# A third pair of K tiles as seven products of sums in the down projections of a two-layer trunk

## The chip, the cores and the metric

The kernel runs on one core of a Trainium2 chip. The metric is the device time of one execution in microseconds; lower is better. TensorE (PE) multiplies, VectorE (DVE) and ScalarE (ACT) do the elementwise work, GpSimd (POOL) and SyncE (SP) mostly issue transfers.

## What is computed

A decoder trunk of two layers over 256 rows of width 2048. Layer 0 mixes by a gated spatial unit and a sparse attention, layer 1 by a short gated convolution; each mixer has an input and an output projection. Every layer then has a feed-forward part, and a last norm ends the trunk. The change concerns the last product of this, with `D_FF` = 5632:

```python
def swiglu(h, w_gate, w_up, w_down):
    return (jax.nn.silu(h @ w_gate) * (h @ w_up)) @ w_down
...
        h = h + swiglu(rmsnorm(h, norm_ffn[i]), w_gate[i], w_up[i], w_down[i])
    return rmsnorm(h, norm_f)
```

All is float32. The kernel splits every operand into a rounded high part and a low rest (`h`, `l`; `wh`, `wl`) and forms each product from three matmuls: high by high, high by low, low by high.

## The kernel before

**Blocks and units.** The 256 rows are two row tiles (`MT` = 2, `m`), K goes in tiles of 128, columns in chunks of 512 (`NW`). A *block* (`Stream.block`) computes two chunks of columns at once: gate and up for one chunk of the hidden width, or two chunks of a down projection. Its K runs over 8 pairs of K tiles (6 in the last part). The blocks are cut into *units*, and `Stream.run` goes through them: `multiply(i)` issues the matmuls of unit i, `ahead(i)` splits the weights of the units up to four further on, and `after(i)` runs what was hooked to this unit.

**Two kinds of pairs.** A pair of K tiles by two row tiles by two chunks is, for each chunk, four products of a 128x128 block of the operand with a 128x512 block of weights: eight in all. An ordinary pair is two units ("n", one for each chunk) with 12 matmuls each. The other kind replaces the eight products by seven (Winograd's form of Strassen's scheme): four units ("s") of 2, 2, 2 and 1 products, that is 6, 6, 6 and 3 matmuls. It needs sums of operand blocks and of weight blocks. The weights' sums are made partly by transfers that add into SBUF (issued by POOL in `load`, L184) and partly by two additions on VectorE (`sum2`, L137; `sum4`, L140); the operand's sums are made in `x_split` (L423 to L439). Which pairs are done so says `SUMS`, pairs 4 and 6; the sums live in the tiles `sa`, `sx` (`open_late`, `second_operand`).

**The order.** A string sets the order of a block's units by hand:

```python
    N8 = [(k, k in SUMS) for k in range(8)], "nnnnn sns sns sns sns nnn"
    F8 = [(k, k in (4, 6)) for k in range(8)], "nnnnnn sns sns sns sns nn"
    N6 = [(k, k in SUMS) for k in range(6)], "nnn nn sn sn sn s nn"
```

An "sns sns" is the first, second, third and fourth unit of one seven with two ordinary units between. N8 is used for blocks of eight pairs, F8 for the first block behind a norm, N6 for down blocks of six pairs.

**PSUM.** Ordinary products and four of a chunk's sums accumulate in the four buffers of `pg` (`BANK`). Four products of sums (P1, P5, P6, P7, keys in `FREE`) have banks of their own in `pm`, which has four buffers too, given out in turn; transposes (`transposed_bank`, L370) take theirs from the same four. P1 is opened by the first unit of a block's first seven, P5 and P7 by its second, P6 by its third; all are held until the block's sums are done.

**End of a block.** When the last seven has multiplied its third unit, `summed` (L464) copies P1 out and adds P5 to P7 on VectorE (L472 to L475); a down block adds the two results to `h` (L503). `done` then adds the ordinary banks to `h` (L508), two for the first chunk behind the block's last unit, two for the second behind the first unit of the next block; the next block's first matmul needs the first of these banks.

**Start of a block.** `begun` hooks the preparation of operands: for the down projections `pairs` transposes the product of silu(gate) and up (L1000) behind units 2 and 3 of the next block, two pairs each gate block, and `x_split` turns each one unit later into `y` (`split_T`, L381, L382) or, for pairs in `SUMS`, into `y` and `sx`.

**Parts.** `feed_forward` takes the hidden width in parts of 4, 4 and 3 chunks (`PARTS`): a part's gate and up blocks, then its down blocks, two for all 2048 columns (one in the very last part, whose other columns go by plain `gemm`). That makes 6 + 5 down blocks, 8 of eight pairs and 3 of six.

**Weights.** `load` issues the transfers on SP in the order of the units as buffers come free (8 of `raw`, two of `ts`); `split` makes high and low parts (L205 on ScalarE, L208 on VectorE) in a ring of five buffers (`wh0` to `wh4`): a unit's split can start when the unit five before it has multiplied.

Of the kernel before, what the change touches and what calls it, by code (L numbers as in the profile page):

```python
# [8 lines left out]
F32 = mybir.dt.float32  # L9
BF16 = mybir.dt.bfloat16  # L10
F32R = mybir.dt.float32r
AF = mybir.ActivationFunctionType
# [3 lines left out]
P = 128  # L16
# [17 lines left out]
PROBS, VALUES = 4, 6  # L34
PARTS = (4, 4, 3)
SUMS = {4: 0, 6: 1}
BANK = ((1, 3), (2, 7))
P1, P5, P6, P7 = FREE = (0, 4, 5, 6)


class Operand:

    def __init__(self, h=None, l=None, sh=None, sl=None):
        self.h, self.l, self.sh, self.sl = h, l, sh, sl

    def tile(self, kt, m):
        sl = slice(m * P, (m + 1) * P)
        return self.h[:, kt, sl], self.l[:, kt, sl]  # L50

    def sum(self, kp, i):
        return self.sh[:, SUMS[kp], i], self.sl[:, SUMS[kp], i]


class Stream:
# [44 lines left out]
    def block(self, ws, form, src, begun, summed, done):  # L101
# [6 lines left out]
        for kp, seven in order:  # L108
# [3 lines left out]
            def t(k, m, k0=k0):  # L112
                return lambda: src.tile(k0 + k, m)

            def s(i, kp=kp):
                return lambda: src.sum(kp, i)

            if not seven:
                for n in range(2):
                    queue["n"].append((wk[n], {"frees": 1, "mms": [(k, t(k, m), BANK[n][m]) for m in range(MT)  # L120
                                                                    for k in range(2)]}))
# [3 lines left out]
        for c in pattern.replace(" ", ""):  # L125
# [4 lines left out]
            elif item:  # L130
# [8 lines left out]
                def sum4(ra=ra, rb=rb, ts=ts):  # L139
                    self.nc.vector.tensor_add(ts[0][:, 2], self.raw[rb][:, 0], self.raw[ra][:, 1])  # L140

                sevens = [
                    {"raw": ra, "prep": sums13, "mms": [(0, t(0, 0), P1), (1, t(1, 0), BANK[0][0])]},
                    {"raw": rb, "ts": ts, "at": 0, "then": sum2, "mms": [(0, s(1), P5), (1, s(0), P7)]},
                    {"raw": rb, "then": sum4, "frees": (ra,), "mms": [(0, s(2), P6), (1, s(3), BANK[1][0])]},
                    {"raw": rb, "ts": ts, "at": 2, "w": 1, "mms": [(0, t(1, 1), BANK[0][1])]},
                ]
# [102 lines left out]
    def run(self):  # L250
        n = len(self.units)
        i = 0
        while i < n:
# [9 lines left out]
            if u.get("first"):  # L263
                c["ps"] = [self.bank(k) for k in BANK[self.turn]]
                self.turn ^= 1
# [25 lines left out]
def trunk(ctx: ExitStack, tc: tile.TileContext, x, norm_mix, norm_ffn, norm_f, w_in_ab, w_out_ab, sgu_w, sgu_b,  # L291
          sgu_g, cmp_pe_k, cmp_w1_k, cmp_w2_k, cmp_pe_v, cmp_w1_v, cmp_w2_v, w_in_c, conv_w, w_out_c, w_gate,
          w_up, w_down, out):
    nc = tc.nc
# [10 lines left out]
    st = Stream(nc, raws, parts, (psg, psm))  # L305
# [5 lines left out]
    h = acts.tile([P, MT, D], F32, name="h")  # L311
# [64 lines left out]
    def split_T(banks, dst, kt0, gain):  # L376
        dh, dl = dst
        for b, t in enumerate(banks):
            k0 = kt0 + 2 * b
            if gain is None:  # L380
                nc.scalar.activation(dh[:, k0:k0 + 2, :], t, AF.Copy)  # L381
                nc.vector.tensor_sub(dl[:, k0:k0 + 2, :], t, dh[:, k0:k0 + 2, :].bitcast(F32))  # L382
            else:
                gs = [gain[:, k0 + k:k0 + k + 1] for k in range(2)]
                for k, g in enumerate(gs):
                    nc.scalar.activation(dh[:, k0 + k, :], t[:, k, :], AF.Copy, scale=g)
                for k, g in enumerate(gs):
                    nc.vector.scalar_tensor_tensor(dl[:, k0 + k, :], t[:, k, :], g, dh[:, k0 + k, :].bitcast(F32),
                                                   op0=ALU.mult, op1=ALU.subtract)
# [21 lines left out]
    late = {}  # L411

    def x_split(src, dst, kp, gain=None):

        ks = slice(2 * kp, 2 * kp + 2)
        if kp not in SUMS:
            split_T([src.rearrange("p (k m) c -> p k (m c)", k=2)], (dst.h, dst.l), 2 * kp, gain)
            return
        xs = late["pool"].tile([P, 8, P], F32, name="xs")
        a = xs[:, :4]  # L420
        if gain is not None:
            for k in range(2):
                nc.scalar.activation(a[:, 2 * k:2 * k + 2], src[:, 2 * k:2 * k + 2], AF.Copy,  # L423
                                     scale=gain[:, 2 * kp + k:2 * kp + k + 1])
        elif src.space == bass.MemoryType.PSUM:
            nc.scalar.activation(a, src, AF.Copy)
        else:
            a = src
        v = a.rearrange("p (k m) c -> p k (m c)", k=2)
        nc.vector.tensor_sub(xs[:, 4:6], a[:, 0:2], a[:, 1:4:2])  # L430
        nc.vector.tensor_sub(xs[:, 6], a[:, 0], xs[:, 5])
        nc.vector.tensor_sub(xs[:, 7], a[:, 2], xs[:, 6])

        def parts():
            i = SUMS[kp]
            nc.scalar.activation(dst.h[:, ks], v, AF.Copy)
            nc.scalar.activation(dst.sh[:, i], xs[:, 4:], AF.Copy)
            nc.vector.tensor_sub(dst.l[:, ks], v, dst.h[:, ks].bitcast(F32))
            nc.vector.tensor_sub(dst.sl[:, i], xs[:, 4:], dst.sh[:, i].bitcast(F32))  # L439

        st.at(1, parts)

# [5 lines left out]
    def open_late():  # L448
        next_region()
        pool = late["pool"] = region("late")  # L450
        pool.tile([P, LATE_PAD], F32, name="pad")
        for n in ("a", "x"):
            for x in "hl":
                late[n + x] = pool.tile([P, len(SUMS), 4, P], F32R, name=f"s{n}_{x}")
        src_a.sh, src_a.sl = late["ah"], late["al"]
        st.widen(pool)

    def second_operand():

        src_x.h, src_x.l = (yp.tile([P, KT, S], F32R, name=f"y{i}") for i in range(2))  # L460
        if late:
            src_x.sh, src_x.sl = late["xh"], late["xl"]

    def summed(part, b):  # L464

# [28 lines left out]
    def add_to_h(n2, squares=None):  # L494
# [10 lines left out]
        def done(n, b):  # L505
            for m in range(MT):
                hs = h[:, m, c0 + n * NW:c0 + (n + 1) * NW]
                nc.vector.tensor_add(hs, b[BANK[n][m]], hs)  # L508
            if squares:
# [7 lines left out]
    def region(name, bufs=1):  # L517
        return stage.enter_context(tc.tile_pool(name=name, bufs=bufs, reuse_waits="tile"))

    def next_region():  # L520
        stage.close()
# [59 lines left out]
    src_a, src_x = Operand(a_h, a_l), Operand()  # L581
# [375 lines left out]

    N8 = [(k, k in SUMS) for k in range(8)], "nnnnn sns sns sns sns nnn"
    F8 = [(k, k in (4, 6)) for k in range(8)], "nnnnnn sns sns sns sns nn"
    N6 = [(k, k in SUMS) for k in range(6)], "nnn nn sn sn sn s nn"  # L960
    begun = []

    f0 = norm_from("f0", g_ffn[0])
# [17 lines left out]
        st.gemm(w_out_ab[0], [0, 8, 12, 4], c * NW, src_x, out_ab(c, *f0))  # L981


    def feed_forward(layer, rname, norm):
        c0 = 0
        for part, nb in enumerate(PARTS):
            for c in range(c0, c0 + nb):
                def done(n, b, c=c, kb=4 * c0):
                    g, u = late["g"], late["u"]
                    for m in range(MT):  # L990
                        t = (g, u)[n][:, m]
                        nc.vector.tensor_add(t, b[BANK[n][m]], t)

                    def later():
                        for m in range(MT):
                            r = R[rname][:, m:m + 1]
                            if n == 0:
                                nc.scalar.activation(g[:, m], g[:, m], AF.Silu, scale=r)
                            else:
                                nc.vector.scalar_tensor_tensor(g[:, m], u[:, m], r, g[:, m], op0=ALU.mult, op1=ALU.mult)  # L1000

                    st.at(1, later)

                def pairs(b, c=c, c0=c0):
                    if c == c0 and b == 0:
                        second_operand()
                    x_pair(late["g"], b * S, src_x, 2 * (c - c0) + b)

                st.block([(w_gate[layer], 0, c * NW), (w_up[layer], 0, c * NW)], F8 if c == 0 else N8, src_a, begun[:],
                         summed, done)  # L1010
                begun[:] = [(2, lambda p=pairs: p(0)), (3, lambda p=pairs: p(1))]
            last = part == len(PARTS) - 1
            for n2 in range(2):
                if last and layer == 1 and n2 == 1:
                    break
                sums, done = add_to_h(n2, norm[0] if last else None)
                ws = [(w_down[layer], 4 * c0, 2 * n2 * NW), (w_down[layer], 4 * c0, (2 * n2 + 1) * NW)]
                st.block(ws, N8 if nb == 4 else N6, src_x, begun[:], sums, done)
                begun[:] = norm[1](n2) if last else []
            c0 += nb  # L1020

# [12 lines left out]


    cv = {}
    top = ExitStack()
    wc = w_in_c[0]

    def open_conv():  # L1040
        cv["p"] = top.enter_context(tc.tile_pool(name="convt", bufs=2, reuse_waits="tile"))
        r2 = cv["r2"] = const.tile([P, MT], F32, name="r2")
        nc.vector.tensor_mul(r2, R["c1"], R["c1"])
# [68 lines left out]
    for c in (0, 2):  # L1112
        for cc in (c, c + 1):
            done, then = done_cz(cc)
# [3 lines left out]
        done, then = done_bg(c)  # L1118
# [4 lines left out]
    for n2 in range(2):  # L1123
        sums, done = add_to_h(n2, squares)
# [68 lines left out]
    for c in (2, 3):  # L1193
        w = w_down[1][4 * sum(PARTS[:2]) * P:]
        st.gemm(w, [0, 4, 8], c * NW, src_x, last(c), tail=AHEAD + 1 if c == 3 else 0)
# [61 lines left out]
```

## Time and profile before

| | |
|---|---|
| median of 3 runs | 2150.6 us (2150.55 to 2150.61) |
| the profiled execution | 2150.6 us |
| its span | 2148.9 us |
| PE busy | 2128.4 us, 99% |
| PE weight loads | 1750.3 us, 81% |
| DVE busy | 1610.4 us, 75% |
| ACT busy | 1146.3 us, 53% |
| POOL busy | 161.0 us, 7% |
| DMA | 473.30 MB, mean 220 GB/s |

The profile is of one execution. Busy time of PE counts the matmuls' modelled durations, which overlap, so it tells that PE has work and not how fast it goes. The chain that ended last runs 96% over PE and 1% each over DVE, DMA and issue. Idle time of another engine costs nothing as long as PE doesn't wait for it.

### The profile page before, as it was taken

The page shows a single profiled execution, that of the slowest core. Times are in us where ns is not written, and L with a number is a line of the kernel's source. Part 1 is how long each engine was busy: PE and PEld are TensorE (multiplying, and loading weights), DVE is VectorE, ACT ScalarE, POOL GpSimd, SP SyncE. Part 2 cuts the span into 40 slices and gives each one's busy share as a digit, 9 for nine tenths or more (in the row PEclk, how much of TensorE's full clock was granted, in tenths as well). Part 3 has the DMA queues.
Part 4 walks back from the last instruction along what each step waited for, and adds up shares of the span by engine and source line. Part 5 has one row for each costly group of instructions (what it writes and reads, how often), then busy time and mean ns, then how long its engine had stood idle before and what let it go on. Part 6 is the DMA issues. An engine that isn't in the chain of part 4 may idle for free.

```text
span 2148.9 us, 27123 instructions
## 1 busy us (share of the span) xinstructions
PE 2128.4 (99%) x9663; PEld 1750.3 (81%) x9663; DVE 1610.4 (75%) x1981; ACT 1146.3 (53%) x1411; POOL 161.0 (7%) x217
## 2 busy tenths in 40 slices
PE   9999999999999999999999999999999999999998
PEld 7887788888888888888788888788888888888886
DVE  5567756777777787777788787877877777777776
ACT  6456555555455555455565555555555455544553
POOL 2000000000000100010010000000000000000000
PEclk9999999999999999999999999999999999999999
DMA  8764467777877877886777777777887788778873
GB/s 261 207 187 129 146 204 208 216 240 230 242 219 241 245 226 216 248 244 200 214 234 221 209 248 238 216 223 219 242 241 220 230 244 241 216 230 244 242 220 108
DMA packets 256040, 473.30 MB, mean 220 GB/s; under 512 B 17848, under 2 KB 29552, under 8 KB 255904
## 3 DMA queue, kind: packets, MB, share of 16 engines
q1 hardware_dynamic: 229104, 425.27, 60.4%
q0 software_dynamic: 23136, 42.67, 12.1%
q10 hardware_dynamic: 3664, 3.63, 0.5%
q8 instruction: 76, 1.25, 0.2%
q14 instruction: 60, 0.49, 0.1%
HBM read 469.40 MB, written 2.10 MB: 219 GB/s over the span
## 4 chain that ended last, share of the span: by engine, by line
PE 96%; DVE 1%; issue 1%; DMA 1%; ACT 1%; SPq 0%; POOLq 0%; POOL 0%; DVEq 0%; ACTq 0%
PE pg L229 23%; PE pg L231 22%; PE pg L230 22%; PE pg L238 5%; PE pg L240 5%; PE pg L239 5%; PE pm L231 3%; PE pm L229 3%; PE pm L230 3%; PE pm L370 2%; DVE wl L208 1%; PE pm L757 0%; PE pm L834 0%; DMA h<-in_x_dram 0%; PE pm L623 0%
## 5 line engine op out<-in xcount | busy, mean ns | idle before, releaser
L208 DVE TENSOR_TENSOR wl<-raw,wh 128x1024 fp32r<-128x1024 f32 (+1 forms) x769 | 928.4, 1221 | 423.6 <-ACT wh L205 392.0
L205 ACT ACTIVATE wh<-raw 128x1024 fp32r<-128x1024 f32 (+1 forms) x769 | 804.7, 1058 | 781.8 <-PE pg L231 525.4
L229 PE MATMUL pg<-wh,a_h 128*128 128x512 f32 x1456 | 572.1, 393 | 1.6 <-DVE h L508 1.6
L231 PE MATMUL pg<-wh,a_l 128*128 128x512 f32 x1456 | 567.4, 390 | 0.0
L230 PE MATMUL pg<-wl,a_h 128*128 128x512 f32 x1456 | 566.8, 389 | 0.0
L229 PEld LDWEIGHTS pg<-wh,a_h 128*128 128x128 f32 x1456 | 273.4, 188 | 58.9 <-ACT wh L205 2.0
L231 PEld LDWEIGHTS pg<-wh,a_l 128*128 128x128 f32 x1456 | 273.3, 188 | 57.7
L230 PEld LDWEIGHTS pg<-wl,a_h 128*128 128x128 f32 x1456 | 273.6, 188 | 55.3
L229 PE MATMUL pg<-wh,y 128*128 128x512 f32 x646 | 253.8, 393 | 3.1 <-DVE h L508 3.1
L231 PE MATMUL pg<-wh,y 128*128 128x512 f32 x646 | 251.7, 390 | 0.0
L230 PE MATMUL pg<-wl,y 128*128 128x512 f32 x646 | 251.4, 389 | 0.0
L205 ACT ACTIVATE wh<-ts 128x1024 fp32r<-128x1024 f32 (+1 forms) x158 | 133.8, 847 | 92.2 <-PE pg L231 91.0
L208 DVE TENSOR_TENSOR wl<-ts,wh 128x1024 fp32r<-128x1024 f32 (+1 forms) x158 | 150.6, 953 | 35.6 <-ACT wh L205 35.6
L184 POOL DMA_DIRECT2D ts<-in_w_up_dram x88 | 76.3, 1015 | 947.0 <-DVE ub L475 324.3
L229 PEld LDWEIGHTS pg<-wh,y 128*128 128x128 f32 x646 | 121.3, 188 | 29.7 <-ACT wh L205 3.9
L231 PEld LDWEIGHTS pg<-wh,y 128*128 128x128 f32 x646 | 121.2, 188 | 25.7
L230 PEld LDWEIGHTS pg<-wl,y 128*128 128x128 f32 x646 | 121.4, 188 | 24.6
L238 PE MATMUL pg<-wh,a_h 128*128 128x512 f32 x288 | 121.0, 420 | 0.6 <-ACT wh L205 0.6
L239 PE MATMUL pg<-wl,a_h 128*128 128x512 f32 x288 | 113.1, 393 | 0.8 <-DVE wl L208 0.8
L240 PE MATMUL pg<-wh,a_l 128*128 128x512 f32 x288 | 113.4, 394 | 0.0
L238 PE MATMUL pg<-wh,y 128*128 128x512 f32 x176 | 69.1, 393 | 1.6 <-DVE h L508 1.6
L240 PE MATMUL pg<-wh,y 128*128 128x512 f32 x176 | 68.5, 389 | 0.0
(255 smaller groups left out, 2188.2 us busy)
## 6 DMA issues: line engine op xcount, KB each, us to landing
raw<-in_w_gate_dram SPq DMA_DIRECT2D x176, 512.0 KB, 4.7
raw<-in_w_down_dram SPq DMA_DIRECT2D x157, 512.0 KB, 5.4
raw<-in_w_up_dram SPq DMA_DIRECT2D x132, 512.0 KB, 4.8
raw<-in_w_in_c_dram SPq DMA_DIRECT2D x84, 512.0 KB, 4.8
raw<-in_w_in_ab_dram SPq DMA_DIRECT2D x72, 512.0 KB, 3.9
ts<-in_w_up_dram POOLq DMA_DIRECT2D x88, 256.0 KB, 5.7
raw<-in_w_out_ab_dram SPq DMA_DIRECT2D x32, 512.0 KB, 4.1
raw<-in_w_out_c_dram SPq DMA_DIRECT2D x28, 512.0 KB, 4.7
```

The lines of the kernel that those rows point to most:

```text
L184: self.nc.gpsimd.dma_start(out=ts[0][:, k], in_=wb[:, 0], accum_op=ALU.add)
L205: nc.scalar.activation(hv[:, ks], src[:, ks], AF.Copy)
L208: nc.vector.tensor_sub(lv[:, ks], src[:, ks], hv[:, ks].bitcast(F32))
L229: nc.tensor.matmul(ps, xh, hv[:, j, :], start=uses[0] == (i, x), stop=False)
L230: nc.tensor.matmul(ps, xh, lv[:, j, :], start=False, stop=False)
L231: nc.tensor.matmul(ps, xl, hv[:, j, :], start=False, stop=uses[-1] == (i, x))
L238: nc.tensor.matmul(ps[m], xh, hv[:, k, :], start=u["first"] and k == 0, stop=False)
L239: nc.tensor.matmul(ps[m], xh, lv[:, k, :], start=False, stop=False)
L240: nc.tensor.matmul(ps[m], xl, hv[:, k, :], start=False, stop=u["last"] and k == 1)
L370: nc.tensor.transpose(t[:, k * S + m * P:k * S + (m + 1) * P], src[:, m, c + k * P:c + (k + 1) * P], ident)
```

## The change

In the down projections pair 2 is done as seven products too, beside pairs 4 and 6 (beside 4 where there are six). Its operand sums go into two new tiles `t0`, `t1` from a pool of their own (`third`), opened at the first part of a layer's feed-forward and closed before the convolution's and at the last norm's. The sums of an operand stand in a dictionary by pair. Gate and up, the convolution and its projections keep their forms. The patterns of the down blocks become D8 and D6:

```diff
+THIRD = 2
...
     def sum(self, kp, i):
-        return self.sh[:, SUMS[kp], i], self.sl[:, SUMS[kp], i]
+        h, l = self.sums[kp]
+        return h[:, i], l[:, i]
...
     def x_split(src, dst, kp, gain=None):
-        if kp not in SUMS:
+        if kp not in dst.sums:
...
-    def second_operand():
+    def second_operand(third=None):
         src_x.h, src_x.l = (yp.tile([P, KT, S], F32R, name=f"y{i}") for i in range(2))
         if late:
-            src_x.sh, src_x.sl = late["xh"], late["xl"]
+            src_x.sums = {kp: (late["xh"][:, i], late["xl"][:, i]) for kp, i in SUMS.items()}
+        if third:
+            src_x.sums[THIRD] = third
...
-    N6 = [(k, k in SUMS) for k in range(6)], "nnn nn sn sn sn s nn"
+    D8 = [(k, k in SUMS or k == THIRD) for k in range(8)], "nn sns sns sns sns sns sns nn"
+    D6 = [(k, k in (4, THIRD)) for k in range(6)], "nn sns sns sns sns nn"
...
                     if c == c0 and b == 0:
-                        second_operand()
+                        if c == 0:
+                            top.close()
+                            pool = top.enter_context(tc.tile_pool(name="third", bufs=1, reuse_waits="tile"))
+                            third[:] = [pool.tile([P, 4, P], F32R, name=f"t{i}") for i in range(2)]
+                        second_operand(third)
...
-                st.block(ws, N8 if nb == 4 else N6, src_x, begun[:], sums, done)
+                st.block(ws, D8 if nb == 4 else D6, src_x, begun[:], sums, done)
```

The lines of the changed kernel are 2 to 12 further on: L208 becomes L210, L229 to L231 become L231 to L233, L370 L372, L382 L384, L472 L476, L503 L507, L508 L512, L1000 L1008.

Two places of the order are shown. The first is VectorE's queue at the end of the first down block (layer 0, first part): `wl` are splits of weights, L503 and L508 the additions to `h`. Before:

```order
L474 TENSOR_TENSOR ub<-pm,ga 128x512
L475 TENSOR_TENSOR ub<-pm,ub 128x512
L503 TENSOR_TENSOR h<-h,ga 128x2x512
L503 TENSOR_TENSOR h<-h,ub 128x2x512
L208 TENSOR_TENSOR wl_4970<-raw,wh_4969 128x1024
L208 TENSOR_TENSOR wl_4988<-raw,wh_4987 128x1024
L208 TENSOR_TENSOR wl_5006<-raw,wh_5005 128x1024
L508 TENSOR_TENSOR h<-pg,h 128x512 x2
```

and with the change:

```order
L478 TENSOR_TENSOR ub<-pm,ga 128x512
L479 TENSOR_TENSOR ub<-pm,ub 128x512
L507 TENSOR_TENSOR h<-h,ga 128x2x512
L507 TENSOR_TENSOR h<-h,ub 128x2x512
L210 TENSOR_TENSOR wl_5017<-raw,wh_5016 128x1024
L210 TENSOR_TENSOR wl_5035<-raw,wh_5034 128x1024
L512 TENSOR_TENSOR h<-pg,h 128x512 x2
```

Between the additions of the sums and those of the ordinary banks stand two splits in place of three; the additions of the next block's first seven (L139, L142) come five rows behind.

The second is TensorE's queue at the start of that same block, from the second transpose of the product (L370, then L372) on; `y` are plain operands, `t` the sums of pair 2, `pg` and `pm` the two groups of PSUM banks, and in brackets stands whom a row waits for. Before, an ordinary unit of twelve matmuls follows, of which seven rows stand here:

```order
L370 MATMUL pm<-ident,ga 128x128 x4
L229 MATMUL pg<-wh_4694,y_3684 128x512 [waits Activation_49]
L230 MATMUL pg<-wl_4695,y_3684 128x512
L231 MATMUL pg<-wh_4694,y_3685 128x512
L229 MATMUL pg<-wh_4694,y_3684 128x512
L230 MATMUL pg<-wl_4695,y_3684 128x512
L231 MATMUL pg<-wh_4694,y_3685 128x512
L229 MATMUL pg<-wh_4694,y_3684 128x512
```

With the change the second and third unit of a seven follow: P5, P7 and, with a wait for VectorE, P6:

```order
L372 MATMUL pm<-ident,ga 128x128 x4
L231 MATMUL pm<-wh_4704,t_3687 128x512 [waits Activation_49]
L232 MATMUL pm<-wl_4705,t_3687 128x512
L233 MATMUL pm<-wh_4704,t_3688 128x512
L231 MATMUL pm<-wh_4704,t_3687 128x512 [waits Activation_49]
L232 MATMUL pm<-wl_4705,t_3687 128x512
L233 MATMUL pm<-wh_4704,t_3688 128x512
L231 MATMUL pm<-wh_4725,t_3687 128x512 [waits DVE_49]
L232 MATMUL pm<-wl_4726,t_3687 128x512
```

The first products of a block's first seven have moved from unit 5 to unit 2, before the transposes, and the three banks of P5, P7 and P6 are opened right behind them.

## Rows read from the trace of the kernel before

**Rows 1.** The page's part 1: busy us, share of the span, instructions by engine.

```profile
PE 2128.4 (99%) x9663; PEld 1750.3 (81%) x9663; DVE 1610.4 (75%) x1981; ACT 1146.3 (53%) x1411; POOL 161.0 (7%) x217
```

**Rows 2.** Windows: engine busy us (x instructions), granted clock, DMA share, GB/s.

```profile
533.30:575.80 42.50, 42.50 (x193) 35.19 (x192) 33.85 (x40) 23.77 (x27) 3.40 (x4) 1.00 0.81 234
1036.00:1042.00 6.00, 4.42 (x21) 3.36 (x20) 6.00 (x8) 3.16 (x6) 0.00 (x0) 1.00 0.84 232
```

**Rows 3.** Timeline of PE, end of an N6 block: start us, us, line, operands.

```profile
1034.48 0.39 PE L231 MATMUL pg<-wh,y 128*128 128x512 f32 x1
...
1037.20 0.39 PE L231 MATMUL pg<-wh,y 128*128 128x512 f32 x1
...
1037.88 0.39 PE L231 MATMUL pg<-wh,y 128*128 128x512 f32 x1
1039.85 0.47 PE L229 MATMUL pg<-wh,y 128*128 128x512 f32 x1 [1.57 <-DVE h L508]
```

**Rows 4.** The waits: who waited for whom, us in total, times, longest.

```profile
PE pg L229 <- DVE h L508: 4.7, 3, 1.6
PE pg L238 <- DVE h L508: 1.6, 1, 1.6
```

**Rows 5.** Timeline of DVE, end of the same N6 block.

```profile
1030.69 1.23 DVE L208 TENSOR_TENSOR wl<-raw,wh 128x1024 fp32r<-128x1024 f32 x1 [0.21 <-ACT wh L205]
...
1036.75 2.35 DVE L208 TENSOR_TENSOR wl<-raw,wh 128x1024 fp32r<-128x1024 f32 x2
1039.02 1.28 DVE L508 TENSOR_TENSOR h<-pg,h 128x512 f32<-128x512 f32 x2
```

**Rows 6.** Timeline of DVE, end of an N8 down block.

```profile
572.30 3.49 DVE L208 TENSOR_TENSOR wl<-raw,wh 128x1024 fp32r<-128x1024 f32 x3
575.70 1.28 DVE L508 TENSOR_TENSOR h<-pg,h 128x512 f32<-128x512 f32 x2
```

**Rows 7.** Timeline of PE, the same end.

```profile
576.16 0.39 PE L231 MATMUL pg<-wh,y 128*128 128x512 f32 x1
576.53 0.47 PE L229 MATMUL pg<-wh,y 128*128 128x512 f32 x1
```

**Rows 8.** Timeline of DVE, end of the F8 block of the output projection.

```profile
1379.41 2.35 DVE L208 TENSOR_TENSOR wl<-raw,wh 128x1024 fp32r<-128x1024 f32 x2
```

**Rows 9.** Timeline of PE, the same end.

```profile
1382.51 0.47 PE L229 MATMUL pg<-wh,y 128*128 128x512 f32 x1 [1.57 <-DVE h L508]
```

**Rows 10.** Timeline of all engines, start of an N8 down block.

```profile
544.63 0.60 PE L370 MATMUL pm<-ident,ga 128*128 128x128 f32 x4
...
544.88 1.06 ACT L205 ACTIVATE wh<-raw 128x1024 fp32r<-128x1024 f32 x1 [1.66 <-issue]
...
545.97 1.23 DVE L208 TENSOR_TENSOR wl<-raw,wh 128x1024 fp32r<-128x1024 f32 x1 [0.40 <-ACT wh L205]
...
547.12 0.68 DVE L382 TENSOR_TENSOR y<-pm,y 128x512 fp32r<-128x512 f32 x1
```

**Rows 11.** Timeline of PE, the same start.

```profile
533.26 0.39 PE L229 MATMUL pg<-wh,y 128*128 128x512 f32 x1
...
544.99 0.48 PE L229 MATMUL pg<-wh,y 128*128 128x512 f32 x1
```

**Rows 12.** Timeline of DVE, the same start.

```profile
538.46 1.41 DVE L1000 SCALAR_TENSOR_TENSOR ga<-ub,r_f,ga 128x512 f32<-128x512 f32 x2
...
548.32 0.69 DVE L439 TENSOR_TENSOR sx_l<-xs,sx_h 128x512 fp32r<-128x512 f32 x1
```

**Rows 13.** DMA: queues (packets, MB, share of engines); issues (KB, us to landing).

```profile
q1 hardware_dynamic: 229104, 425.27, 60.4%
q0 software_dynamic: 23136, 42.67, 12.1%
...
ts<-in_w_down_dram SPq DMA_DIRECT2D x38, 256.0 KB, 6.2
ts<-in_w_down_dram POOLq DMA_DIRECT2D x38, 256.0 KB, 6.7
```

More of the change, by code (lines that the diff above doesn't have):

```diff
@@ L41, with __init__ @@
 class Operand:
-    def __init__(self, h=None, l=None, sh=None, sl=None):
-        self.h, self.l, self.sh, self.sl = h, l, sh, sl
+    def __init__(self, h=None, l=None):
+        self.h, self.l, self.sums = h, l, {}
     def tile(self, kt, m):
@@ L434, in parts @@
         def parts():
-            i = SUMS[kp]
+            sh, sl = dst.sums[kp]
             nc.scalar.activation(dst.h[:, ks], v, AF.Copy)
-            nc.scalar.activation(dst.sh[:, i], xs[:, 4:], AF.Copy)
+            nc.scalar.activation(sh, xs[:, 4:], AF.Copy)
             nc.vector.tensor_sub(dst.l[:, ks], v, dst.h[:, ks].bitcast(F32))
-            nc.vector.tensor_sub(dst.sl[:, i], xs[:, 4:], dst.sh[:, i].bitcast(F32))
+            nc.vector.tensor_sub(sl, xs[:, 4:], sh.bitcast(F32))
         st.at(1, parts)
@@ L454, in open_late @@
                 late[n + x] = pool.tile([P, len(SUMS), 4, P], F32R, name=f"s{n}_{x}")
-        src_a.sh, src_a.sl = late["ah"], late["al"]
+        src_a.sums = {kp: (late["ah"][:, i], late["al"][:, i]) for kp, i in SUMS.items()}
         st.widen(pool)
-    def second_operand():
+    def second_operand(third=None):
         src_x.h, src_x.l = (yp.tile([P, KT, S], F32R, name=f"y{i}") for i in range(2))
         if late:
-            src_x.sh, src_x.sl = late["xh"], late["xl"]
+            src_x.sums = {kp: (late["xh"][:, i], late["xl"][:, i]) for kp, i in SUMS.items()}
+        if third:
+            src_x.sums[THIRD] = third
     def summed(part, b):
@@ L981, in trunk @@
         st.gemm(w_out_ab[0], [0, 8, 12, 4], c * NW, src_x, out_ab(c, *f0))
+    top = ExitStack()
+    third = []
     def feed_forward(layer, rname, norm):
@@ L1036, in trunk @@
     cv = {}
-    top = ExitStack()
     wc = w_in_c[0]
     def open_conv():
+        top.close()
         cv["p"] = top.enter_context(tc.tile_pool(name="convt", bufs=2, reuse_waits="tile"))
```

## The prediction, made before the changed kernel had run

> **What bounds the kernel now.** I read the page first. TensorE's matmuls cover 99% of the span [rows 1], and the windows say the clock is granted in full (1.00, the 2.4 GHz level) in the down projections, while VectorE is busy 33.85 of 42.50 us and the DMA engines 0.81 of it [rows 2]. So only two things change the time: the number of matmuls, and the moments when TensorE stands. The pace of the matmuls is in the timeline: the last matmul of one K-pair unit starts at 1034.48 and that of the next at 1037.20, so twelve matmuls of 512 columns take 2.72 us, **0.2267 us each** [rows 3]. The 0.39 us that the rows give as a duration overlaps the next one and is no price.
>
> The waits say where TensorE stands in the chunks with products of sums: four times at a block's end, for `h` of L508, 6.3 us in all [rows 4]. One of them is the row at 1039.85 [rows 3]: that matmul starts 1.97 us after the one before, 1.74 us more than the pace. The timeline of VectorE explains it [rows 5]: the last split before the sums starts at 1030.69, then come the sums of products and their additions to h, from 1036.75 two splits, and only at 1039.02 the additions that free the PSUM banks for the next block. VectorE doesn't idle in this; the order of its queue is what makes TensorE wait. Where three ordinary units stand behind the last product of sums (N8), VectorE does three splits before those additions, from 572.30 [rows 6], and TensorE meets the free bank almost in time: 576.16 to 576.53 is 0.37 us, 0.14 over the pace [rows 7]. The first chunk of the convolution's output projection (F8 with additions to h) ends on two ordinary units and has again two splits and the 1.57 us of idle time [rows 8, 9]. So **the tail "nn" or "nnn" of the pattern decides**, not the layer: one unit less gives TensorE 2.72 us less to do and VectorE one split (1.13 us, half of the time from 1036.75 to 1039.02) less, and the difference, 1.59 us, is the wait that appears.
>
> **The change, part by part.**
>
> *Products.* Each of the 11 down blocks (8 of eight pairs, 3 of six) does one more pair with seven products in place of eight: 3 matmuls fewer, 33 in all, on the path: 33 x 0.2267 = **-7.5 us**. The Trainium skill's page "TensorE: Matmul & The Clock Gate", section "Back-to-back issue gap", gives N/2.4 + 2.5 ns between matmuls, 215.8 ns at 512 columns; by it the term would be an estimated 7.1 us, but the trace's own pace decides.
>
> *Ends of blocks.* N8 ends on "nnn"; D8, which takes its place in 8 down blocks, ends on "nn". The order shows VectorE's queue with two splits before the additions, as at 1036.75. From the end of the last product of sums TensorE has the same units as there (three ordinary ones and the short fourth unit of the seven), so I take the wait seen there: 1.97 in place of 0.37 us between the matmuls, 8 x 1.60 = **+12.8 us**. N6 ended on "nn" already and D6 does too: those 3 blocks keep theirs. Bounds: 0 if VectorE came to its sums earlier; I take the upper end, for three ends of the same shape all show it.
>
> *Starts of blocks.* The first down block of each part (6: four D8, two D6) transposes the last two pairs of y behind its units 2 and 3. `pm` has four buffers. N8 has only ordinary units there; in D8 and D6 unit 2 is already a product and holds a buffer until the block's end, the transposes take two, P5 the fourth, P7 the first transpose's, and **P6, with which unit 5 opens, the second transpose's**. The order shows a wait for VectorE on its first matmul. What that waits for can be timed in the block of before [rows 10]: the second transpose starts at 544.63, when unit 3 ends; ScalarE first splits the weights whose ring slot unit 3 has just freed (544.88), VectorE follows (545.97), and only then comes L382, which reads the transposed bank, from 547.12 to 547.80: 3.17 us after the end of unit 3, with about 0.15 until TensorE starts (the first of the two additions from 1039.02, 0.68 long like L382, lets the matmul go at 1039.85 [rows 3, 5]). TensorE has there only the transposes, 0.36 us until 544.99 [rows 11] with 0.09 more on the next matmul, and the six matmuls of unit 4, 1.36: 1.81 us. The wait is 3.32 - 1.81 = 1.5 us, 6 x 1.5 = **+9.1 us**. Bounds: 0 (the transposed bank is read before the split) and 2.7 (another split of 1.13 stands ahead); the row is the same work in the same order, so I take its value. The first transposes need L1000's product: in before it ends at 539.87, 6.61 us after the block's start at 533.26 [rows 11, 12], and the thirty matmuls of D8's units 0 to 2 end at 6.80: just in time, 0.
>
> *Operands.* Pair 2 of y is made six times as sums: three subtractions and one split more on VectorE, two copies more on ScalarE, in the third gate block of a part, behind units 3 and 4. The down block of before does just this with pair 6 (L439, its last step, ends at 549.0 [rows 12]) and TensorE doesn't wait; N8's five ordinary units cover it. Cost 0; if the cover failed, as much as a start, 6 x 1.5.
>
> *Splits and additions of weights.* A seven needs 3.5 splits of full width where a pair needs 2, and two additions: VectorE 1.5 x 1.23 + 2 x 0.68 = 3.2 us more [rows 5, 10] in a block of some 42, from 33.85 to 37; TensorE's time in that block covers it, since the inner "sns sns" is what before already runs with without a wait. Cost 0, if it is evenly spread; that it isn't is the ends' term.
>
> *Transfers.* A seven loads 0.26 MB more by SP and adds 0.52 MB by POOL. At the queues' rates (425.27 MB in 60.4% of the span, 42.67 MB in 12.1% [rows 13]) that is 0.8 and 3.2 us of all sixteen engines: the share goes from 0.81 to 0.90. `ts` has two buffers, so the third seven of a block must wait for the fourth unit of the first (unit 7), whose split follows the end of unit 2 by 2.5 us at most (544.63 to 547.12 [rows 10]): 9.3 us into the block. The loads take 6.2, the adding transfers 6.7 [rows 13]: 22.2. Unit 16, which uses them, multiplies behind 132 matmuls, at 29.9 + 2.4 for transposes and wait, so its addition and split must begin at 29. So 0, with 6.8 us to spare; from there each us costs 8, at twice the latencies 8 x 6.1 = 49, the bound above.
>
> **Sum:** -7.5 + 12.8 + 9.1 = +14.4 us. The profiled execution took 2150.6 us (span 2148.9), the median of the three runs is the same 2150.6, so the forecast is **2165.0 us**. The new stops are of the length of those that exist; around one of them the clock stays at 1.00 [rows 2], so none is charged for the clock.
>
> **Rivals.**
> - *Only the ends wait* (the transposed bank is read early enough): -7.5 + 12.8 = 2155.9. For it: ScalarE's copy of the bank comes right behind the wait's start. Against: the order has VectorE's split ahead of L384. 12%.
> - *Only the starts wait:* 2152.2. It needs VectorE ahead of the ends by 1.6 us, which no "nn" end of before is. 5%.
> - *Faster: no new wait.* The mechanism is the ring of five split buffers: if the sevens, which begin three units earlier, let VectorE finish the products' sums of the end before the last splits, the additions to h meet TensorE as in N8, and the bank of P6 is met likewise; then the 33 matmuls count in full, 2143.1. The point from which it decides: the first addition of L512 must start before the block's last matmul (575.70 against 576.16 in N8, but 1039.02 against 1037.88 in N6 [rows 3, 5 to 7]). Against it: the last split before the sums waits for a slot that TensorE frees, and its place hasn't moved. 6%.
> - *The third pair of sums comes late.* It needs more than 6.8 us over the measured latencies; a share of 0.90, with bursts in it, speaks for it, the 22.2 against 29 us against. Price: at 8 us over, 1.2 late in 8 blocks, 2165 + 10 = 2175. The Trainium skill's page "SBUF — State Buffer", section "SBUF: two separate sides", has a rule that would bring this about: descriptors of transfers issued by GpSimd can't be written while VectorE, in a two-port mode, holds the ports that both share. No row here shows it: the adding transfers land in 6.7 us beside a VectorE that is busy 80% of the time. 9%.
> - *The change does not do what it says:* the order has 33 matmuls fewer and 22 adding transfers more; excluded.
> The forecast's own case keeps 68%.
>
> **How the numbers follow.** In the forecast's case the ends are 8 x 1.5 to 1.65, the starts 6 x 1.2 to 1.9, so 2162 to 2168.5. The range takes in the rival of the ends alone below and part of late sums above: 2155 to 2171, with the rest (6 + 5 + most of 9%) outside. About 0.2%, 4.3 us, is what a measurement can tell from no change: slower are the forecast, the ends alone (+5.3) and late sums, 89%; the same is 5%; faster 6%.
>
> **What would show it.** Right: 33 matmuls fewer; gaps of 1.97 us at all eight D8 ends with L512 as releaser, twelve waits of that kind in the list in place of four; six gaps of some 1.7 us on the first P6 matmul with L384 as releaser; VectorE near 88% in a D8 block, clock 1.00. Wrong: an end gap of 0.4 us in a D8 block, no wait for L384, or waits for `ts` transfers on VectorE or ScalarE that reach TensorE.

## The result, and the profile of the changed kernel

| | before | after |
|---|---|---|
| median of the runs | 2150.61 us (4 runs, 2150.55 to 2151.02) | 2164.73 us (4 runs, 2164.64 to 2166.34) |
| ratio, 95% interval | | 1.0064 (1.0052 to 1.0077) |
| profiled execution | 2150.6 us, span 2148.9 | 2166.34 us, span 2164.6 |

The change makes the kernel 14.1 us slower by the medians, where 14.4 were forecast. The profiled execution of after is the longest of its four; the last section says what is peculiar to it.

The page's part 1 of after, to be held against [rows 1]:

```profile
PE 2123.8 (98%) x9630; PEld 1744.9 (81%) x9630; DVE 1650.4 (76%) x2049; ACT 1168.8 (54%) x1445; POOL 179.9 (8%) x239
```

TensorE has 33 matmuls fewer (9663 to 9630) and 4.6 us less busy time, and the span is 15.7 us longer. So the time has gone into stops, and the list of waits says which (who waited for whom: us in total, times, longest; rows of other waits are left out):

```profile
PE pg L231 <- DVE h L512: 17.6, 11, 1.9
PE pm L231 <- DVE y L384: 7.3, 6, 1.2
...
PE pg L240 <- DVE h L512: 1.6, 1, 1.6
...
PE pm L372 <- DVE a_l L390: 0.6, 1, 0.6
```

Twelve waits for the additions to h (L512) stand where [rows 4] had four, the six waits for the transposed bank (L384) are new, and one short wait for L390 too.

A D8 end, TensorE's timeline at the end of the first down block of the second part:

```profile
839.22 0.39 PE L232 MATMUL pg<-wl,y 128*128 128x512 f32 x1
839.45 0.39 PE L233 MATMUL pg<-wh,y 128*128 128x512 f32 x1
841.41 0.47 PE L231 MATMUL pg<-wh,y 128*128 128x512 f32 x1 [1.57 <-DVE h L512]
```

and VectorE's at the same place:

```profile
832.25 1.22 DVE L210 TENSOR_TENSOR wl<-raw,wh 128x1024 fp32r<-128x1024 f32 x1 [0.20 <-ACT wh L207]
833.39 0.68 DVE L476 TENSOR_TENSOR ub<-pm,ga 128x512 f32<-128x512 f32 x1
...
837.17 1.22 DVE L507 TENSOR_TENSOR h<-h,ub 128x1024 f32<-128x1024 f32 x1
838.31 2.35 DVE L210 TENSOR_TENSOR wl<-raw,wh 128x1024 fp32r<-128x1024 f32 x2
840.58 1.28 DVE L512 TENSOR_TENSOR h<-pg,h 128x512 f32<-128x512 f32 x2
```

Behind the split of 832.25 no row of VectorE has idle time in brackets: it works through four sums, two additions of the sums and two splits, and comes to L512 at 840.58, 1.13 us after TensorE's last matmul has started. In N8 it came to these additions 0.46 us before TensorE's last matmul started [rows 6, 7]. Seven of the eight D8 ends show 1.96 us between the two matmuls; the first shows 2.24.

A start, in the same block. ScalarE first:

```profile
805.98 1.06 ACT L207 ACTIVATE wh<-raw 128x1024 fp32r<-128x1024 f32 x1 [2.09 <-issue]
806.95 0.58 ACT L383 ACTIVATE y<-pm 128x512 fp32r<-128x512 f32 x1
```

VectorE:

```profile
807.08 1.23 DVE L210 TENSOR_TENSOR wl<-raw,wh 128x1024 fp32r<-128x1024 f32 x1 [1.76 <-DMA ts<-in_w_down_dram]
808.22 0.68 DVE L384 TENSOR_TENSOR y<-pm,y 128x512 fp32r<-128x512 f32 x1
```

TensorE, from the second transposes to the first matmul of P6 and the one behind it:

```profile
805.74 0.60 PE L372 MATMUL pm<-ident,ga 128*128 128x128 f32 x4
...
807.34 0.40 PE L233 MATMUL pm<-wh,t 128*128 128x512 f32 x1
808.96 0.51 PE L231 MATMUL pm<-wh,t 128*128 128x512 f32 x1 [1.22 <-DVE y L384]
809.30 0.39 PE L232 MATMUL pm<-wl,t 128*128 128x512 f32 x1
```

The gap is 1.62 us and the next one 0.34, two matmuls at the pace of [rows 3] are 0.45: **1.51 us** lost, at all six starts within 0.01. The order on ScalarE and VectorE is that of [rows 10]: split, copy, split, then L384. (The name behind VectorE's 1.76 us, a transfer, is the profile's guess; the split follows ScalarE's of 805.98, which it needs.)

### The profile page after: what moved, and what is told of

Read it like the earlier page. It is cut to its first block, busy times and chain, and to the rows that moved or that the text cites. A ratio compares the mean times of both kernels' runs of the same rounds, so it can differ in the third digit from the quotient of the medians.

```text
span 2164.6 us, 27273 instructions
## 1 busy us (share of the span) xinstructions
PE 2123.8 (98%) x9630; PEld 1744.9 (81%) x9630; DVE 1650.4 (76%) x2049; ACT 1168.8 (54%) x1445; POOL 179.9 (8%) x239
## 4 chain that ended last, share of the span: by engine, by line
PE 89%; DVE 4%; issue 3%; DMA 2%; ACT 2%; SPq 0%; POOLq 0%; POOL 0%; DVEq 0%; ACTq 0%
PE pg L231 20%; PE pg L233 20%; PE pg L232 20%; PE pg L240 5%; PE pg L242 5%; PE pg L241 5%; PE pm L231 3%; PE pm L233 3%; PE pm L232 3%; DVE wl L210 2%; PE pm L372 2%; DMA ts<-in_w_down_dram 2%; ACT wh L207 1%; PE pm L761 0%; PE pm L838 0%
## 5 line engine op out<-in xcount | busy, mean ns | idle before, releaser
L210 DVE TENSOR_TENSOR wl<-raw,wh 128x1024 fp32r<-128x1024 f32 (+1 forms) x769 | 928.3, 1222 | 411.7 <-ACT wh L207 381.8
L231 PE MATMUL pg<-wh,a_h 128*128 128x512 f32 x1456 | 572.1, 393 | 7.9 <-DVE h L512 7.9
L233 PE MATMUL pg<-wh,a_l 128*128 128x512 f32 x1456 | 567.4, 390 | 0.0
L231 PEld LDWEIGHTS pg<-wh,a_h 128*128 128x128 f32 x1456 | 273.4, 188 | 65.2 <-ACT wh L207 9.8
L233 PEld LDWEIGHTS pg<-wh,a_l 128*128 128x128 f32 x1456 | 273.2, 188 | 57.6
L231 PE MATMUL pg<-wh,y 128*128 128x512 f32 x580 | 228.1, 393 | 9.7 <-DVE h L512 9.7
L233 PE MATMUL pg<-wh,y 128*128 128x512 f32 x580 | 226.6, 391 | 0.0
L232 PE MATMUL pg<-wl,y 128*128 128x512 f32 x580 | 226.3, 390 | 0.0
L207 ACT ACTIVATE wh<-ts 128x1024 fp32r<-128x1024 f32 (+1 forms) x180 | 152.4, 847 | 97.3 <-PE pg L233 95.3
L210 DVE TENSOR_TENSOR wl<-ts,wh 128x1024 fp32r<-128x1024 f32 (+1 forms) x180 | 171.4, 952 | 23.5 <-ACT wh L207 23.5
L231 PEld LDWEIGHTS pg<-wh,y 128*128 128x128 f32 x580 | 109.3, 188 | 34.3 <-ACT wh L207 12.1
L233 PEld LDWEIGHTS pg<-wh,y 128*128 128x128 f32 x580 | 109.2, 188 | 23.1
L232 PEld LDWEIGHTS pg<-wl,y 128*128 128x128 f32 x580 | 109.4, 189 | 22.3
L186 POOL DMA_DIRECT2D ts<-in_w_down_dram x60 | 51.9, 989 | 447.0 <-DMA ts<-in_w_down_dram 233.8
L240 PE MATMUL pg<-wh,y 128*128 128x512 f32 x176 | 69.1, 393 | 1.6 <-DVE h L512 1.6
```

Source lines behind the costliest of these rows:

```text
L186: self.nc.gpsimd.dma_start(out=ts[0][:, k], in_=wb[:, 0], accum_op=ALU.add)
L207: nc.scalar.activation(hv[:, ks], src[:, ks], AF.Copy)
L210: nc.vector.tensor_sub(lv[:, ks], src[:, ks], hv[:, ks].bitcast(F32))
L231: nc.tensor.matmul(ps, xh, hv[:, j, :], start=uses[0] == (i, x), stop=False)
L232: nc.tensor.matmul(ps, xh, lv[:, j, :], start=False, stop=False)
L233: nc.tensor.matmul(ps, xl, hv[:, j, :], start=False, stop=uses[-1] == (i, x))
```

## Experiments

All were timed in three rounds beside the kernel before (2150.9 to 2151.0 us there; the ratios are to that). Medians scatter by some tenths. The program's start scatters too: TensorE waits 1.7 to 2.7 us there for x and up to 1.6 us for a first split, and the first down block begins between 532.9 and 534.9 us in the twelve traces (533.15 in that of after). So the gaps between matmuls decide next to the median.

**1. D8 with N8's tail.**

```
-    D8 = ... "nn sns sns sns sns sns sns nn"
+    D8 = ... "nn sns sns sns sns ss sns nnn"
```

> The changed kernel, with D8's last product of sums laid out as N8's (the third unit of the last seven, one ordinary unit, the fourth unit, three ordinary units); the start and D6 stay, the products are the same. Theory (the tail sets what VectorE has queued ahead of the additions): the eight D8 ends fall from 1.97 us to about 0.4 us between two matmuls, the six starts stay, so 2164.7 - 8 x 1.59 = 2152.0 us. Rival (VectorE is simply too full in a D8 block, wherever the units stand): the wait stays or comes up inside the block, 2160 to 2165 us. Second rival (the third pair of sums is then late, one unit earlier and without an ordinary unit inside it): waits for a ts transfer or a split in the middle, 2155 to 2162 us.

Measured: 2153.32 us (2152.43 to 2154.31), ratio 1.001 (1.0 to 1.0019). All eight D8 ends are 0.38 to 0.39 us, the six starts 1.62 as in after, and no new wait stands inside a block. VectorE now has three splits ahead of L512 and is in time:

```profile
831.06 3.49 DVE L210 TENSOR_TENSOR wl<-raw,wh 128x1024 fp32r<-128x1024 f32 x3
834.47 1.28 DVE L512 TENSOR_TENSOR h<-pg,h 128x512 f32<-128x512 f32 x2
```

and on TensorE:

```profile
834.92 0.39 PE L233 MATMUL pg<-wh,y 128*128 128x512 f32 x1
835.30 0.47 PE L231 MATMUL pg<-wh,y 128*128 128x512 f32 x1
```

The profiled execution (2152.43 us) is 0.4 us over the forecast of 2152.0, and its first down block begins 0.5 us later than that of after (533.69); what the median has above that, 0.9 us, no trace shows. Both rivals fall, the late third pair too, though it is asked for a unit earlier here.

**2. An ordinary unit ahead of P6's unit.**

```
-    D8 = ... "nn sns sns sns sns sns sns nn"
-    D6 = ... "nn sns sns sns sns nn"
+    D8 = ... "nn snsnss sns sns sns sns nn"
+    D6 = ... "nn snsnss sns sns nn"
```

> The changed kernel, with one ordinary unit of the first seven moved from behind P6's unit to ahead of it, in D8 and D6; the tails stay. Theory (TensorE waits 1.4 us for the bank of the second transpose, which VectorE reads 3.2 us after unit 3): 2.72 us more work stand between, so the six waits for L384 go, 2164.7 - 6 x 1.39 = 2156.4 us, with the twelve waits for L512 unchanged. Rival (VectorE's backlog is what TensorE meets there, not the one read): a wait of 1 to 1.5 us appears on one of the next units, 2163 to 2165 us.

Measured: 2158.61 us (2157.18 to 2160.09), ratio 1.0034 (1.0021 to 1.0047). No wait for L384 is left, the twelve for L512 stand. One new one is there, at one start: the transposes wait 0.3 and 0.4 us for the product,

```profile
PE pm L372 <- DVE ga L1008: 0.7, 2, 0.4
```

so "just in time" is all that the first transposes are. The forecast was 2156.4: the profiled execution, 2157.18 us, is over it by just about this new wait, and the median's further 1.4 us stand in executions without a trace. The rival (VectorE's backlog met on a next unit) falls.

**3. Both moves.**

```
+    D8 = ... "nn snsnss sns sns ss sns nnn"
+    D6 = ... "nn snsnss sns sns nn"
```

> The changed kernel with both moves in D8 (an ordinary unit ahead of P6's unit, N8's tail), and D6 with the first move alone. Theory (two separate waits, both set by where ordinary units stand): the gains add, 2164.7 - 12.7 - 8.4 = 2143.6 us, which is the time before less the 33 products (2143.1) and 0.5 us; four waits for L512 are left, the three of D6 and one of the convolution's output projection. Rival (with ten ordinary units in a D8 block the inside is too thin: two sevens follow each other almost without one): 1 to 2 us in each of eight blocks come back inside, 2151 to 2160 us.

Measured: 2144.21 us (2143.12 to 2147.49), ratio 0.9969 (0.9957 to 0.9981). The two gains add (2143.6 was forecast), and the changed kernel is faster than the kernel before, by 6.4 us on the medians of the result and by 6.8 within these rounds. The products alone would give 7.5; the trace begins its first down block 0.8 us later than that of before (534.07 against 533.26).

**4. The kernel before, with the tail "nn" in its down blocks.**

```
-                st.block(ws, N8 if nb == 4 else N6, src_x, ...)
+                st.block(ws, F8 if nb == 4 else N6, src_x, ...)
```

> The kernel before, its down blocks of eight pairs with F8's pattern in place of N8's: the same two sevens and the same products, one ordinary unit moved from the end to the start. Theory (the tail alone makes the wait, with or without a third seven): eight ends of 1.97 in place of 0.37 us, 2150.6 + 8 x 1.59 = 2163.3 us, and no wait at a start. Rival (the third seven's work on VectorE and the queues makes it): no change, 2150.6 us.

Measured: 2164.84 us (2162.78 to 2165.03), ratio 1.0061 (1.0044 to 1.0077). With two sevens and not one matmul more or fewer, the eight ends go to 1.96 us (the 1.5 us over the forecast of 2163.3 stand at the program's start, in this trace 1.6 us longer than in that of before):

```profile
838.28 0.39 PE L231 MATMUL pg<-wh,y 128*128 128x512 f32 x1
840.24 0.47 PE L229 MATMUL pg<-wh,y 128*128 128x512 f32 x1 [1.58 <-DVE h L508]
```

The third pair has no part in the end's wait; the place of one ordinary unit makes it.

**5. Three ordinary units at the very end, but the third and fourth unit of the seven together.**

```
-    D8 = ... "nn sns sns sns sns sns sns nn"
+    D8 = ... "nn sns sns sns sns sns ss nnn"
```

> The changed kernel, with the ordinary unit between the third and the fourth unit of the last seven moved behind the fourth: D8 ends on three ordinary units, but TensorE has the same 39 matmuls behind the last third unit as before the move. Theory (the wait is TensorE's work behind the third unit against VectorE's queue behind it: splits, sums, splits, additions): both sides are unchanged, the eight ends stay at 1.97 us, 2164.7 us. Rival (three ordinary units at the end are enough, as the prediction put it by the letters of the tail): 8 x 1.59 us go, 2152.0 us.

Measured: 2166.48 us (2165.3 to 2166.81), ratio 1.0071 (1.0056 to 1.0086). The eight ends are those of after (seven of 1.96, the first of 2.24), and VectorE has the same two splits ahead of L512. The 1.8 us over 2164.7 are in the trace a slow stretch behind the first end, of which the last section tells, and a start 0.4 us longer. So it is not the letters at the end but TensorE's work behind the last third unit: 39 matmuls in D8 and here, 51 in N8 and in experiment 1.

**6. The bank read ahead of the split, patterns untouched** (at the six starts).

```
+            for fn in self.early.pop(i, []):
+                fn()
             self.ahead(i)
...
+        if early:
+            st.early.setdefault(st.at_unit + 1, []).append(lambda: x_split(t, dst, kp, gain))
```

> The changed kernel with its patterns as they are; only in the first down block of each part ScalarE and VectorE read the second transposed bank ahead of the split of weights that stood in front (in the program's order, one place on each engine). Theory (the wait at P6 is this one split standing ahead of L384): the six gaps fall from 1.62 to 0.25 to 0.5 us, 2164.7 - 6 x 1.1 to 1.39 = 2156.4 to 2158 us. Rival (the copy of the bank and the three subtractions of pair 6 take the time anyway, or the delayed split is missed four units later): 2162 to 2165 us.

Measured: 2159.1 us (2157.83 to 2159.47), ratio 1.0035 (1.0022 to 1.0048). The six gaps are 0.41 and 0.34 us, 0.29 over two matmuls:

```profile
805.91 0.40 PE L234 MATMUL pm<-wh,t 128*128 128x512 f32 x1
806.32 0.51 PE L232 MATMUL pm<-wh,t 128*128 128x512 f32 x1
806.66 0.40 PE L233 MATMUL pm<-wl,t 128*128 128x512 f32 x1
```

So 1.22 us of each 1.51 were that one place in two queues. By this the run should take 2157.4; the trace has the slow stretch of the last section besides, 1.6 us. VectorE's rows of the same start:

```profile
805.57 0.69 DVE L387 TENSOR_TENSOR y<-pm,y 128x512 fp32r<-128x512 f32 x1 [1.69 <-ACT y L386]
806.52 1.23 DVE L211 TENSOR_TENSOR wl<-raw,wh 128x1024 fp32r<-128x1024 f32 x1 [0.26 <-ACT wh L208]
```

No wait for the delayed split shows in the list.

**7. The first half's additions ahead of the splits, patterns untouched** (all eleven down ends).

```
-        self.soon[end - 1] = lambda: done(0, chunk["banks"])
+        early = pattern.startswith("nn s")
+        self.soon[end - 1 - early] = lambda: done(0, chunk["banks"])
+        if early:
+            self.hold.add(end - 3)
...
-            self.ahead(i)
+            if i not in self.hold:
+                self.ahead(i)
```

> The changed kernel with its patterns as they are; at the end of a down block VectorE makes the first two additions to h (L512) ahead of the two splits that stood in front of them, as soon as the last ordinary unit of the first half is through, in all eleven down blocks. Theory (these two splits, 2.3 us, are the wait): the eight D8 and three D6 ends fall from 1.97 to 0.23 to 0.4 us, 2164.7 - 11 x 1.59 to 1.74 = 2145.6 to 2147.2 us; the starts stay. Rival (the splits are then late for the next block's first units, by the 1.3 us that the additions take): a wait for wl at the next block's second or third unit takes most of it back, 2155 to 2163 us.

Measured: 2159.59 us (2159.22 to 2161.03), ratio 1.0041 (1.0026 to 1.0056). This is a miss: the wait moved by one unit. VectorE,

```profile
835.70 1.28 DVE L517 TENSOR_TENSOR h<-pg,h 128x512 f32<-128x512 f32 x2
836.90 3.48 DVE L214 TENSOR_TENSOR wl<-raw,wh 128x1024 fp32r<-128x1024 f32 x3
840.30 1.28 DVE L517 TENSOR_TENSOR h<-pg,h 128x512 f32<-128x512 f32 x2
```

and the first unit of the next block goes at the pace, but the second, which needs the other half's banks, starts after a gap of 1.57 us:

```profile
839.56 0.39 PE L237 MATMUL pg<-wh,y 128*128 128x512 f32 x1
841.13 0.47 PE L235 MATMUL pg<-wh,y 128*128 128x512 f32 x1 [1.19 <-DVE h L517]
```

I had looked at the first addition only; behind it three splits now stood ahead of the second pair of additions. Ten of the eleven ends do so (the first 1.84 us); the last, ahead of plain `gemm`, has no gap. At five of the ten the list names a split of ScalarE instead of L517. I read them as the same wait, for the matmul starts 0.15 us after the first L517 has ended there (883.93 to 884.08) as here.

**8. All four additions ahead of the splits.** From experiment 7 on:

```
-        self.soon[end] = lambda: done(1, chunk["banks"])
+        self.soon[end - early] = lambda: done(1, chunk["banks"])
         if early:
-            self.hold.add(end - 3)
+            self.hold |= {end - 3, end - 2}
```

> The changed kernel with its patterns as they are; at the end of a down block VectorE makes all four additions to h (both halves) ahead of the splits that stood in front of and between them, in eleven blocks. The run with the first half moved alone left 1.57 us at the second unit, where three splits stood ahead of the second half. Theory (VectorE's queue between the sums and the second unit of the next block holds two or three splits, which nobody needs before that unit): splits come 838.5 to 841.9 on that run's clock, the first needed by 839.8, so 0 to 0.4 us are left at each end, 2164.7 - 11 x 1.2 to 1.6 = 2147 to 2151.5 us. Rival (VectorE is full at a block's end by the whole wait, and the order only says which unit meets it): 1 us or more comes up at the second or third unit for wl, 2157 to 2164 us.

Measured: 2145.74 us (2145.16 to 2147.66), ratio 0.9976 (0.9966 to 0.9986), better than the 2147 to 2151.5 expected. No gap over 0.3 us is left at any of the eleven ends; VectorE:

```profile
832.86 2.47 DVE L517 TENSOR_TENSOR h<-pg,h 128x512 f32<-128x512 f32 x4
835.26 3.48 DVE L214 TENSOR_TENSOR wl<-raw,wh 128x1024 fp32r<-128x1024 f32 x3
```

The splits, 2.4 us later, come in time. So VectorE is not too full at a block's end; it did work first that nobody yet needed. (The one wait for L390, at the four transposes, grows to 1.8 us in exchange.)

**9. All tails mended in the patterns**, for the fastest version: D8 as in experiment 3, and

```
-    F8 = ... "nnnnnn sns sns sns sns nn"
-    D6 = ... "nn sns sns sns sns nn"
+    F8 = ... "nnnnnn sns sns ss sns nnn"
+    D6 = ... "nn snsnss ss sns nnn"
```

> Patterns alone, going for a version faster than both: D8 as in the run with both moves, D6 with N8's tail too (its first product of sums then has no ordinary unit to the end of the first seven), and F8 (the first chunk of each gate pair and of the convolution) with N8's tail. Theory: four more ends without a wait, three of D6 and one of the convolution, 2144.2 - 4 x 1.59 = 2137.8 us. Rival (seven units of sums with one ordinary unit among them are too dense for VectorE, 3.5 splits and two additions per 21 matmuls): waits for wl in D6 and F8 of 1 us or more, 2141 to 2148 us.

Measured: **2137.05 us** (2136.41 to 2137.73), ratio 0.9934 (0.9917 to 0.995): 13.8 us faster than before in the same rounds, 27.7 faster than the change as it was made, with the same products. No wait for L384 or L512 is in its list; all ends are 0.37 to 0.38 us.

**10. The kernel before with its tails mended**, to price the third pair alone:

```
-    F8 = ... "nnnnnn sns sns sns sns nn"
-    N6 = ... "nnn nn sn sn sn s nn"
+    F8 = ... "nnnnnn sns sns ss sns nnn"
+    N6 = ... "nnnnn ssnsns nnn"
```

> The kernel before, with two sevens in a down block of eight pairs as it was; only F8 and N6 get N8's tail (F8 by moving one inner ordinary unit to the end, N6 by drawing its one seven together). It tells what the third pair is worth once no end waits, in the comparison with the version that has all patterns mended (2137.05 us). Theory: the four old waits of 1.59 us go, 2150.6 - 6.4 = 2144.2 us, and the difference to that version is the 33 products, 7.5 us, less 0.5 for a short wait at the four transposes of the last part: 7.0. Rival (the mended version gains from something else, and the third pair's sums, splits and loads cost TensorE a part of the 7.5): 2138 to 2142 us, a difference of 1 to 5 us.

Measured: 2144.42 us (2144.06 to 2147.61), ratio 0.9971 (0.996 to 0.9983). Against experiment 9 the third pair is worth 2144.42 - 2137.05 = 7.4 us: the 33 products, with nothing given back for its sums, splits, additions and loads that stands out of the scatter of some tenths.

## Why the prediction was right

Both kinds of new stops are where the forecast put them, with the releasers that it named; term by term:

- *Products, -7.5 us.* 33 matmuls are gone, and experiments 9 and 10 give 7.4 us for them.
- *Ends, +12.8 us.* The gaps go from 0.38 to 1.96 us at seven ends and to 2.24 at the first; counted as eight of a kind, 8 x 1.58 = 12.7 us. Experiment 4 makes the same wait without the third pair, 1 takes it away by the place of units, 8 by VectorE's order. One wording was too simple: "the tail 'nn' or 'nnn' of the pattern decides". Experiment 5 ends on "nnn" and waits all the same; the count of TensorE's units behind the last product of sums, which the prediction's paragraph on the ends gives, was the right one.
- *Starts, +9.1 us.* 6 x 1.51 = 9.1. Experiment 2 removes it with one ordinary unit more in between, and experiment 6 takes 1.22 of each 1.51 with one place in the queues. Inside the sum two small parts were off and made up for each other: P6's first matmul starts 0.06 us after L384 has ended, not 0.15, and the next one loses 0.11 more.
- *Operands, splits, transfers, 0.* Experiment 10 against 9 bears this out. For the third `ts` the step can be read: its loads were issued at 850.15, 8.7 us into the block that began at 841.41 (9.3 forecast), the later of its adding transfers at 854.69 with 8.4 us to landing, so 21.7 us into the block (22.2 forecast), and its addition on VectorE began at 865.08 with no idle time ahead of it. But the 6.8 us to spare were right for a part's first block alone: the second, like this one, has neither the transposes nor the start's wait, so the spare time is 2.4 us less there, 4.4 by the prediction's own figures. The rival of late sums is out, also where the sums were asked for earlier (experiments 1, 3 and 9).
- *First transposes, 0.* Held in the kernel as changed, with 0.19 us to spare at all six starts (1614.61 + 1.41 = 1616.02 for the product here):

```profile
1614.61 1.41 DVE L1008 SCALAR_TENSOR_TENSOR ga<-ub,r_f,ga 128x512 f32<-128x512 f32 x2
1616.21 0.60 PE L372 MATMUL pm<-ident,ga 128*128 128x128 f32 x4
```

Experiment 2 lost 0.7 us at one start of six, so the margin was as thin as the text said.
- *What the sum lacked.* One D6 block also makes the four transposes of the next norm, and the second two wait for their bank (L390 above): 0.6 us. Against that, two old waits at the starts of the last part (1020.03 and 2087.07 in before, 0.24 us each over the pace) are gone. -7.5 + 12.7 + 9.1 + 0.6 - 0.5 = +14.4, where the medians give 14.1. That the two terms that it lacked cancel is luck. The upper end of the case's spread was added up wrongly: 8 x 1.65 and 6 x 1.9 give 2167.7, not 2168.5, which changes nothing here.
- *VectorE near 88% of a D8 block* was wrong. The windows of a second down block, VectorE alone (stretch, its length, busy us and instructions, granted clock, DMA share, GB/s), before and then after:

```profile
576.53:618.97 42.44, 32.28 (x35) 1.00 0.78 231
```

```profile
841.41:884.73 43.32, 35.13 (x39) 1.00 0.85 243
```

It is 35.13 of 43.32, 81%, and 2.85 us more than before, not 3.2. My base of 33.85 [rows 2] was that of a part's first block, with the splits of y in it. For the first block ahead of this one the 37 us of work came out, but the two new stops lengthen it, so the share is 82%:

```profile
795.72:841.41 45.69, 37.39 (x45) 1.00 0.81 237
```

The DMA share rose by 0.07 in the second block (0.78 to 0.85), where 0.09 were forecast. Nothing in the sum hung on these shares, and they show how little a share says: with VectorE idle for 8.2 us in the second block, TensorE waited for it at the end.

## To carry to other kernels

An engine that is idle a fifth of the time can still hold up the busiest one, when its queue does early work ahead of the one instruction that frees a bank: read, at each place where a bank changes hands, what stands ahead of that instruction, and move it or give the waiting engine more work. When an order is changed, follow both halves of the handover: moving only the first two additions moved the wait by one unit (experiment 7), moving all four removed it (experiment 8). And price a change that saves work by its neighbours too: these 33 products were worth 7.4 us, the places of a few units 28, some of them in blocks that the change hadn't touched.

## What was not expected

- *The clock after one of twelve stops.* In the profiled execution of after, 1.6 us after TensorE has gone on from the first D8 end, matmuls start every 0.427 us instead of 0.227:

```profile
580.74 0.63 PE L231 MATMUL pg<-wh,y 128*128 128x512 f32 x1
581.16 0.63 PE L232 MATMUL pg<-wl,y 128*128 128x512 f32 x1
```

The window of that stretch, and one behind the same end of the second part, TensorE alone:

```profile
580.74:583.73 2.99, 2.99 (x9) 0.50 0.85 288
841.41:846.40 4.99, 4.99 (x22) 1.00 0.99 234
```

The granted clock is 0.50 there, the 1.2 GHz level, for 3 us, about 1.6 us lost. That is the size of this execution's surplus over the other three (1.6 to 1.7 us), of which there is no trace. The stretch came back in experiments 5 and 6, which have the same first end of 2.24 us, and not in experiment 2, which has it too; all stops of 1.96 us left the clock at 1.00. So "none is charged for the clock" holds for eleven ends of twelve. What decides at the first wasn't tried.
- *Why that end is 0.28 us longer:* ScalarE stood idle for 0.58 us before its second split ahead of the sums, where every other block has 0.30, and VectorE's queue came 0.28 us later by it. The profile names the same releaser in both cases, so what held it stays open.
- *The adding transfers land later with the third pair, the plain loads of `ts` sooner.* Issue to landing of `ts` in the down projections was 6.2 us (plain) and 6.7 us (adding) [rows 13]; with 60 transfers of each kind in place of 38:

```profile
ts<-in_w_down_dram SPq DMA_DIRECT2D x60, 256.0 KB, 4.9
ts<-in_w_down_dram POOLq DMA_DIRECT2D x60, 256.0 KB, 7.4
```

It is so in every run: 7.1 to 7.6 us for the adding ones in the nine with 60, 6.0 to 6.7 in the three with 38, and 4.6 to 5.2 against 6.2 to 6.3 for the plain ones. The plain loads of whole weights (512 KB) went the other way, 5.8 to 6.1 us against 5.2 to 5.4. Why wasn't tried.
